# Attention loop of a hybrid decoder layer: last unit's scaling ahead of copies, next scores behind its transposes, weight splits behind the exponentials, two gate weights off GpSimd

## The chip, the cores and the metric

The kernel runs on one NeuronCore of a Trainium2 chip. Five engines work side by side, each through its own queue in order: TensorE (PE; matrix products and transposes, results in PSUM), VectorE (DVE), ScalarE (ACT), GpSimd (POOL), and SyncE (SP), which here only issues DMA transfers. They meet through semaphores. The metric is the device time of one execution in microseconds (us); the median of several runs counts.

## The reference

One layer of a hybrid decoder, on a prompt of 2048 tokens and on 8 sequences of 8 new tokens (64 sample tokens). The model width is 1024.

```python
h = rms_norm(x, g_mix_pre)
proj = jnp.einsum('btd,de->bte', h, w_in)     # 8 q heads, 2 k, 2 v heads of 64; GLA q, k, v, gate; low rank gate
q = rope(q, pos); k = rope(k, pos)
attn = swa_banded(q, k, v, sinks)             # window 128: each block of 128 queries sees 256 keys
o, s_new = gla_chunked(gq, gk, gv, log_a, s_init)
o = rms_norm(o, g_gla) * jax.nn.silu(gr)
x = x + rms_norm(concat([attn, o]) @ w_out, g_mix_post)
h = rms_norm(x, g_ffn_pre)
x = x + rms_norm(relu(h @ w_up) ** 2 @ w_down, g_ffn_post)
```

The outputs are both activations, the last keys and values of each sequence, and the states of the gated linear attention (GLA). The change touches the stage that does the first projection (q, k, v and the low rank gate) and the sliding-window attention; its softmax is

```python
m = jnp.maximum(jnp.max(scores, axis=-1, keepdims=True), sink)
p = jnp.exp(scores - m)
return p / (jnp.sum(p, axis=-1, keepdims=True) + jnp.exp(sink - m))
```

## The kernel before, in words

**Precision.** Products run in a fast 32-bit format that rounds its operands. To keep the result exact enough, an operand is split into a high part (a ScalarE copy into that format) and a low part (a VectorE subtraction: source minus high part), and a product is made of two or three matmuls (high by high, high by low, low by high). So nearly every operand costs one ScalarE copy and one VectorE subtraction: xh and xl for x, ph and pl for the softmax weights, qh and ql for the two halves of q, kh and kl for k, vv for v, wg for the gate weights.

**The attention loop** (from line 794 on) runs over 16 blocks i of 128 tokens. A block has four units u = 0 to 3; a unit is two query heads of one key head (`unit`, line 465). A unit goes through the steps: a copy of the sink (POOL), scores `sc` (four matmuls), masking with minimum (two VectorE operations, s<-sc), exponentials (two on ScalarE, with the row sum in `den`), reciprocal and scaling of s (for units 0 and 3 one head is scaled on ScalarE and one on VectorE, for units 1 and 2 both on VectorE), four transposes `pT`, the copy ph (ScalarE), the subtraction pl (VectorE), the product `av` with v (four matmuls), the copy `rest` (ScalarE) and the sum `mo` (VectorE).

The steps are written as a Python generator. In pass u the loop draws the steps of three units in turn: `behind` (the unit before, from pl to mo), `now` (from masking to ph) and `ahead` (the scores of the next unit). Between them it runs `fill`, the projection matmuls of a later block, so many as `A_FILL[u]` says in three places, 48 in a block.

**Order.** What is called through `te`, `ac` and `dv` (TensorE, ScalarE, VectorE) is chained by the class `InOrder`, so these three queues hold exactly the order in which the loop makes the calls. POOL's and SP's instructions are called plainly; a scheduler at build time places them by readiness in its own model, so POOL can start work that the loop writes later.

**Work beside the units.** It is put in by name and phase through `A_PLAN` and `do(u, phase)`; a phase is a letter, and "3A" means unit 3, phase A (behind the exponentials), "S" is behind the scaling, "B" behind the transposes, "C" behind ph, "T" behind the masking:

- `x_half(i + 3, u)` for u = 0 and 1: four transposes xT of x and their high part xh; the low part xl is the step `x0` or `x1`. It is there for i up to 13.
- `heads_T(i + 1)` in unit 2: transposes pq (q) and pk (k), their high parts, and the steps `klo0`, `klo1` (low parts of k), `lo0`, `lo1` (low parts of q on VectorE: qh<-pq and ql<-pq), `hi1` (ScalarE, ql<-pq). `lo0`, `hi1` and `klo0` are done in unit 3; `lo1` and `klo1` in unit 0 of the next block. Scores of units 0 and 1 need lo0, those of units 2 and 3 need lo1.
- `take_first(i + 2)` and `take_rest(i + 2)` (`first`, `rest`): a finished projection is taken from PSUM on ScalarE (qk, glr, vv), with the low parts of vv and glr on VectorE as step `vl`.
- `rotate(i + 1)` (`turn`): rotary embedding on POOL, five operations (tb, tb, qk, rot, rot).
- `x_norm(i + 3)` (`junk`, `rstd`): square sums.

**PSUM.** `bank` (line 168) hands out eight banks: two each of the kinds a (projections), b (scores and pk), c (pT), and one each of d and e. Kind d is used by the transposes of x and by pq, kind e by av:

```python
return ps.tile(shape, F32, tag=kind, name=name, bufs=1 if kind in "de" else 2)
```

**Gate weights.** From block 3 on two pieces of the GLA weights (chunks 0 and 1, eight pieces k each) are loaded per block into two buffers `wg_raw`, and `split_some` splits them (`split_gw`, line 257): POOL multiplies by the gain, ScalarE copies the high part, POOL subtracts for the low part. Chunks 2 and 3 (`G_LATE`), split in block 15 and later, use `split_gained`: ScalarE copies with the gain as scale, VectorE multiplies and subtracts in one operation, and POOL does nothing.

After the loop come the sample tokens, the GLA, the output projection and the MLP; nothing of them is changed.

Of the kernel before, what the change touches and what calls it, by code (L numbers as in the profile page):

```python
# [25 lines left out]
NB = T // P  # L26
# [26 lines left out]
H_FETCH = ((6, 6), (1, 0), (1, 8), (5, 0), (5, 8), (3, 0), (3, 8))  # L53
H_EARLY, H_LATE = (1, 2), (5, 7, 6, 4, 3)
G_EARLY, G_LATE = (0, 1), (2, 3)
A_FILL = ((11, 2, 0), (10, 0, 2), (10, 0, 0), (12, 1, 0))
A_LEAD, A_SPLIT = 14, (2, 1, 0, 0)
A_PLAN = [(name, (int(at[0]), at[1])) for name, at in dict(
    klo0="3T", first="1B", hi1="3C", x1="1B", lo1="0A", klo1="0B", x0="0C", rest="3A", lo0="3A", junk="2A", turn="1A", rstd="1A", vl="3S"
).items()]  # L60
G_FIRST = (0, 1)
G_NEXT = (NB, *range(2, NB))
G_ORDER = (0, 1, 2, 3)
G_FILL = (34, 14, 16, 8, 20)
# [51 lines left out]
def f32(ap):  # L116
    return ap.bitcast(F32)
# [23 lines left out]
def hybrid_step_kernel(ctx: ExitStack, tc: tile.TileContext, I, O):  # L141
# [79 lines left out]
    def split_gained(wh, wl, raw, k):  # L221

        g = gcol[:, k : k + 1]
        ac.activation(wh, raw, AF.Copy, scale=g)
        dv.scalar_tensor_tensor(wl, raw, g, f32(wh), op0=ALU.mult, op1=ALU.subtract)
# [22 lines left out]
    def open_gw(chunks):  # L248
        p_ = open_pool(f"g_w{chunks[0]}", "right")
        for c in chunks:  # L250
            gw[c] = (p_, *(p_.tile([P, KT, G_N], F32R, tag=f"w{c}{u}", name=f"wg{c}_{u}") for u in range(2)))
        return p_

    def load_gw(c, k, *stage):
        return c, k, load_raw(sp, k, G_AT + c * G_N, G_N, f"wg{c}", *stage)

    def split_gw(c, k, raw):
        if c in G_LATE:
            split_gained(gw[c][1][:, k, :], gw[c][2][:, k, :], raw, k)
            return  # L260
        nc.gpsimd.tensor_tensor(raw, raw, gcol[:, k : k + 1].to_broadcast([P, G_N]), op=ALU.mult)
        ac.activation(gw[c][1][:, k, :], raw, AF.Copy)
        nc.gpsimd.tensor_tensor(gw[c][2][:, k, :], raw, f32(gw[c][1][:, k, :]), op=ALU.subtract)
# [19 lines left out]
    def load_x(i):  # L283
        xs_in[i] = x = sp.tile([P, D], F32, tag="x", name=f"x_{i}", bufs=2)
        nc.sync.dma_start(x[: rows(i)], x_rows(i))
        ropes[i] = sp.tile([P, 2, HD], F32, tag="rope", name=f"rope_{i}", bufs=4)
        nc.sync.dma_start(ropes[i], I["c_rope"][i])
# [32 lines left out]
    def store():  # L320

        for dst, src in stores:
            nc.sync.dma_start(dst, src)
        stores.clear()
# [274 lines left out]
    def load_T(i, xT):  # L599
        for u in range(2):  # L600
            dst = xT[1][:, :, u * NS : (u + 1) * NS] if i == NB else xT[u]
            nc.sync.dma_start(f32(dst), xt_d[i][:, u])
        return xT
# [24 lines left out]
    def load_cache(name, c):  # L628
        t = sp.tile([P, 4, P], F32, tag=f"cache_{name}", name=f"c{name}_{c}", bufs=1)
        nc.sync.dma_start(t, I[f"cache_{name}"][0, c * 4 : c * 4 + 4].rearrange("b w h d -> w b (h d)"))  # L630
        return t

    def load_consts():

        raw = [gp_pool.tile([P, G_W], F32, tag="gp", name=f"c_raw{u}", bufs=2) for u in range(2)]
        nc.sync.dma_start(raw[1][:, : I["c_rest"].shape[1]], I["c_rest"])
        gk, extra = raw[0][:, :256], raw[0][:, 256:512]
        nc.gpsimd.memset(raw[0][:, :512], 0.0)
        for r0 in (0, HD):
            for a in range(3):  # L640
                nc.sync.dma_start(gk[r0 + a * 16 : r0 + a * 16 + 16], I["w_gk2"][0])
            nc.sync.dma_start(gk[r0 + 48 : r0 + 49], I["b_gk"])
            nc.sync.dma_start(extra[r0 + 49 : r0 + 50], I["b_gk"])
        wgk = kp.tile([P, 2, 256], F32R, name="wgk")
        nc.gpsimd.memset(f32(wgk), 0.0)
        for u, rr in enumerate(half_of):
            nc.scalar.activation(wgk[rr, u], gk[rr], AF.Copy)
            lo = slice(u * HD + 32, u * HD + HD)
            nc.vector.tensor_tensor(gk[lo], gk[lo], f32(wgk[lo, u]), op=ALU.subtract)
            nc.vector.tensor_tensor(wgk[lo, u], gk[lo], extra[lo], op=ALU.add)  # L650
        at = [0]

        def part(n, shape, dtype):
            t = kp.tile([n, *shape], dtype, name=f"c_{at[0]}")
            w = int(np.prod(shape))
            src = raw[1][:n, at[0] : at[0] + w]
            nc.vector.tensor_copy(t.rearrange("p a b -> p (a b)") if len(shape) > 1 else t, src)
            at[0] += w
            return t

        msk = part(P, [NL - 1, P // 4], U8)
        smsk = part(NS, [SL, NS // 2], U8)
        onehot = part(NS, [DB], F32)
        dmsk = kp.tile([P, HD], U8, name="dmsk")
        nc.vector.tensor_tensor(dmsk, ident[:, :HD], ident[:, HD:], op=ALU.add)
        ggla = bcast(kp, I["g_gla"][0], P, "ggla")
        return wgk, msk, smsk, dmsk, onehot, ggla
# [95 lines left out]
    def split_some(n):  # L763

        for _ in range(min(n, len(weights))):
            c, k, raw, stage = weights.popleft()
            split_gw(c, k, raw)
            if stage and late:
                weights.append((*load_gw(*late.popleft(), *stage), stage))
# [20 lines left out]
    now, ahead, behind = next(queue), next(queue), iter(())  # L790
# [3 lines left out]
    for i in range(NB):  # L794
        if i + 4 < NTILE:
            load_x(i + 4)
        if i == NB - 1:
            wa_pool.release()
            w_pools.append(open_gw(G_LATE))
            for n in range(4):  # L800
                stage = ("w_raw", 2) if n % 2 else ("x", 2)
                weights.append((*load_gw(*late.popleft(), *stage), stage))
        elif i >= 3:
            for _ in range(min(2, len(early))):
                weights.append((*load_gw(*early.popleft()), None))
        store()
        if i == 4:
            nc.sync.dma_start(gain_d.rearrange("a d -> (a d)"), I["g_mix_post"][0])
            wgk, msk, smsk, dmsk, onehot, ggla = load_consts()
        if i == NB - 4:  # L810
            nc.sync.dma_start(smask, I["c_smask"])
            cached.update({(name, 0): load_cache(name, 0) for name in "kv"})
        if i >= NB - 2:
            t = i - NB + 2
            gxTs[t] = load_T(t, x_place(t))
            fill = chain(fill, projecting(t, gxTs[t], G_EARLY, ac))
        new = i + 3 < NTILE
        todo["turn"] = lambda: run(rotate(i + 1))
        if i + 2 < NTILE:
            todo["first"] = lambda: take_first(i + 2)  # L820
            todo["rest"] = lambda: todo.update(vl=take_rest(i + 2))
        if new:
            todo["junk"] = lambda: todo.update(rstd=x_norm(i + 3))

        def do(u, phase):
            for name, at in A_PLAN:
                if at == (u, phase) and name in todo:
                    todo.pop(name)()

        for u in range(4):  # L830
            next(now)
            do(u, "T")
            next(behind, None)
            next(now)
            do(u, "A")
            later = next(queue)
            next(later)
            run(fill, A_FILL[u][0])
            next(behind, None)
            if u != 3:  # L840
                next(behind, None)
            run(fill, A_FILL[u][1])
            if u == 0:
                next(now)
            if u < 2 and new:
                hi, todo[f"x{u}"] = x_half(i + 3, u)
                hi()
            elif u == 2:
                todo.update(heads_T(i + 1))
            do(u, "X")  # L850
            run(fill, A_FILL[u][2])
            if u:
                next(now)
            do(u, "S")
            if u == 3:
                next(behind, None)
            next(behind, None)
            next(ahead)
            next(now)
            do(u, "B")  # L860
            split_some(A_SPLIT[u] if i < NB - 1 else 1)
            next(now)
            do(u, "C")
            behind, now, ahead = now, ahead, later
    for left in todo.values():
        left()
    store()
    fill = chain(fill, *(projecting(t, gxTs[t], G_LATE, ac) for t in G_FIRST))

# [20 lines left out]
    for n in range(4):  # L890
# [23 lines left out]
        behind, now, ahead = now, ahead, later  # L914
# [447 lines left out]
    def products():  # L1362

        xT = {G_NEXT[0]: load_T(G_NEXT[0], x_place(G_NEXT[0]))}
        for i, after in zip(G_NEXT, (*G_NEXT[1:], None)):
            if after is not None:
# [517 lines left out]
    turn = [0]  # L1884
# [304 lines left out]
```

## Time and profile before

| | |
|---|---|
| median of 3 runs | 2207.52 us (2206.16 to 2207.61) |
| profiled execution | 2206.11 us, span of the instructions 2204.0 us |
| granted TensorE clock, mean | 0.996 |
| TensorE busy | 2163.2 us, 98% of the span |
| VectorE, ScalarE, GpSimd busy | 1531.4, 1219.1, 263.0 us |
| attention loop, about 37.8 to 300 us | TensorE 256.3, VectorE 226.2, ScalarE 222.7, GpSimd 152.7 us busy of 262.2 |

A timeline row gives the start in us from the span's first instruction, the duration, the engine, the line (L130 is the helper through which the three ordered queues call), the operation, the tiles (out<-in, without buffer numbers), the shapes, and how many like instructions were merged (x2). In brackets stands the idle time before it and what ended it. A matmul's record is longer than the distance to the next one, because matmuls are pipelined; so for TensorE the distances from start to start are read. The loop's blocks are alike: in a steady block, unit 2 with pq is at 232.7 us, unit 3 from 234.1, unit 0 of the next block from 238.1, unit 1 from 242.3.

### The profile page before, as it was taken

Reading aid. Unit: us, or ns where it says so; the run is one execution under the profiler, and the core shown is the slowest. Engines: PE = TensorE matmul, PEld = TensorE weight load, DVE = VectorE, ACT = ScalarE, POOL = GpSimd, SP = SyncE. Lnnn points to the kernel's source line nnn. Section 1 sums busy time; section 2 is a strip of 40 time slices with the busy share of each in tenths; the row PEclk is TensorE's granted clock in tenths of the full one; section 3 lists DMA queues with packets and bytes.
Section 4 is the critical chain, followed back from the end, with each engine's and each line's share of the span. In section 5 each row is a group of like instructions: output and inputs, shape, how many; then the busy total and the mean of one; then the engine's idle time right before and its main releaser. Section 6 shows DMA issues by size and latency. Waiting matters only on the chain.

```text
span 2204.0 us, 34115 instructions
## 1 busy us (share of the span) xinstructions
PE 2163.2 (98%) x11784; PEld 1864.7 (85%) x11784; DVE 1531.4 (69%) x3101; ACT 1219.1 (55%) x2626; POOL 263.0 (12%) x418
## 2 busy tenths in 40 slices
PE   8999999999999999899999999999999999999998
PEld 7999989999998888688888887887888888888886
DVE  5888868777775665788888655547676666555566
ACT  5889867566664444555555544435444554444444
POOL 2566512121111100000000000000000000000000
PEclk9999999999999999999999999999999999999999
DMA  6344232214336665768777677758554334766685
GB/s 228 131 137 156 96 106 70 68 64 148 136 125 237 223 208 190 239 228 277 260 261 270 232 236 225 240 182 260 180 195 149 138 144 148 238 201 193 194 269 185
DMA packets 240185, 411.53 MB, mean 187 GB/s; under 512 B 25924, under 2 KB 142124, under 8 KB 235900
## 3 DMA queue, kind: packets, MB, share of 16 engines
q1 hardware_dynamic: 240012, 409.35, 55.9%
q8 instruction: 93, 1.52, 0.3%
q14 instruction: 80, 0.66, 0.1%
HBM read 265.82 MB, written 143.99 MB: 186 GB/s over the span
## 4 chain that ended last, share of the span: by engine, by line
PE 85%; DVE 6%; ACT 4%; DMA 2%; issue 1%; POOL 1%; SPq 0%; DVEq 0%; ACTq 0%; POOLq 0%
PE dn L130 26%; PE gproj L130 10%; PE uc L130 7%; PE ua L130 7%; PE out L1318 6%; PE proj L130 5%; PE ue L130 4%; PE ud L130 4%; PE ub L130 4%; PE av L130 1%; PE sam L130 1%; PE dsam L130 1%; PE o L130 1%; PE pT L130 1%; PE sc L130 1%
## 5 line engine op out<-in xcount | busy, mean ns | idle before, releaser
L130 PE MATMUL dn<-o0t,o0s 128*128 128x512 f32 x896 | 349.3, 390 | 2.8 <-DVE f L1891 1.5
L130 PE MATMUL dn<-o1t,o0s 128*128 128x512 f32 x896 | 349.5, 390 | 0.3 <-DVE o1t L219 0.2
L130 PE MATMUL dn<-o0t,o1s 128*128 128x512 f32 x896 | 349.4, 390 | 0.0
L219 DVE TENSOR_TENSOR o1s<-rs,o0s 128x512 fp32r<-128x512 f32 x224 | 154.7, 691 | 227.8 <-ACT o0s L218 223.7
L218 ACT ACTIVATE o0s<-rs 128x512 fp32r<-128x512 f32 x224 | 141.1, 631 | 305.5 <-PE dn L130 282.3
L130 PE MATMUL gproj<-wg,gxh 128*128 128x384 f32 x1024 | 272.5, 342 | 0.3 <-DVE gp_s L213 0.3
L130 ACT ACTIVATE st<-st 128x512 f32<-128x512 f32 x224 | 141.2, 630 | 140.7 <-DVE st L130 136.6
L130 PEld LDWEIGHTS dn<-o0t,o0s 128*128 128x128 f32 x896 | 168.3, 188 | 40.6 <-DVE f L1891 2.4
L130 PEld LDWEIGHTS dn<-o1t,o0s 128*128 128x128 f32 x896 | 168.2, 188 | 37.0 <-DVE o1t L219 1.1
L130 PEld LDWEIGHTS dn<-o0t,o1s 128*128 128x128 f32 x896 | 168.2, 188 | 35.0
L130 PEld LDWEIGHTS gproj<-wg,gxh 128*128 128x128 f32 x1024 | 183.8, 188 | 4.1 <-issue 3.1
L130 PE MATMUL uc<-H,s 128*128 128x512 f32 x768 | 186.8, 391 | 0.4 <-DVE s L130 0.4
L130 PE MATMUL gproj<-wg,gxl 128*128 128x384 f32 x576 | 186.0, 340 | 0.2 <-DVE gp_s L213 0.2
L130 PE MATMUL ua<-H,w 128*128 128x512 f32 x744 | 179.2, 390 | 0.0
L130 PEld LDWEIGHTS uc<-H,s 128*128 128x128 f32 x768 | 142.9, 188 | 31.2 <-DVE s L130 0.8
L130 PEld LDWEIGHTS ua<-H,w 128*128 128x128 f32 x744 | 139.7, 188 | 29.5
L1318 PE MATMUL out<-wo,mt 128*128 128x512 f32 x680 | 158.6, 392 | 0.0
L219 DVE TENSOR_TENSOR o1t<-rt,o0t 128x512 fp32r<-128x512 f32 x224 | 153.5, 685 | 7.0 <-ACT o0t L218 6.9
L208 POOL TENSOR_TENSOR frs<-rs_v,half 128x1 f32<-128x1 f32 (+1 forms) x13 | 10.1, 787 | 1214.4 <-DVE rs_v L206 694.5
L1318 PEld LDWEIGHTS out<-wo,mt 128*128 128x128 f32 x680 | 126.5, 188 | 26.1
L218 ACT ACTIVATE o0t<-rt 128x512 fp32r<-128x512 f32 x224 | 138.3, 618 | 8.9 <-DMA rt<-t_d 7.2
L130 DVE TENSOR_TENSOR st<-st 128x512 f32<-128x512 f32 x160 | 110.6, 692 | 27.0 <-ACT st L130 22.6
(405 smaller groups left out, 4322.3 us busy)
## 6 DMA issues: line engine op xcount, KB each, us to landing
s_d<-st SPq DMA_DIRECT2D x32, 1792.0 KB, 8.7
rs<-s_d SPq DMA_DIRECT2D x224, 256.0 KB, 2.8
raw<-in_w_up SPq DMA_DIRECT2D x64, 512.0 KB, 4.3
rt<-t_d SPq DMA_DIRECT2D x128, 256.0 KB, 4.1
rt<-in_w_down SPq DMA_DIRECT2D x96, 256.0 KB, 3.1
t<-in_w_down SPq DMA_DIRECT2D x64, 256.0 KB, 4.0
t_d<-t SPq DMA_DIRECT2D x32, 512.0 KB, 3.2
hraw<-h_d SPq DMA_DIRECT2D x20, 512.0 KB, 5.1
```

What stands on the lines that cost most here:

```text
L130: ins = call(*a, **k)
L208: nc.gpsimd.tensor_tensor(out, v[:n], e, op=ALU.pow)
L218: nc.scalar.activation(hi, src, AF.Copy)
L219: vector.tensor_tensor(lo, src, f32(hi), op=ALU.subtract)
L1318: te.matmul(banks[c], x, w[:, c * 512 : (c + 1) * 512], start=k + u == 0, stop=k == KT - 1 and u == len(products) - 1,)
```

## The change

Five things are moved or replaced; what is computed stays.

1. In unit 3 the scaling comes ahead of `take_rest` and `lo0` (steps `rest` and `lo0` from "3A" to "3S"), and the scores of the next unit come behind the transposes of unit 3 instead of ahead of them.
2. Two of unit 0's eleven first projection matmuls go to unit 3, between av and the transposes.
3. `lo1` goes from "0A" (ahead of unit 0's scaling) to "0S" (behind it, and behind the transposes of x in the order of the calls), and `x0` from "0C" to "1A", behind pl of unit 0; in block 0 it stays.
4. The splits of gate weights go from behind the transposes to behind the exponentials, and from units 0 and 1 (two and one) to units 1 and 2; block 15 keeps its place.
5. Pieces 2 and 3 of chunk 0, which are split in block 4, use `split_gained`.

```diff
-A_FILL = ((11, 2, 0), (10, 0, 2), (10, 0, 0), (12, 1, 0))
-A_LEAD, A_SPLIT = 14, (2, 1, 0, 0)
+A_FILL = ((9, 2, 0), (10, 0, 2), (10, 0, 0), (12, 3, 0))
+A_LEAD, A_SPLIT = 14, (0, 2, 1, 0)
 A_PLAN = [(name, (int(at[0]), at[1])) for name, at in dict(
-    klo0="3T", first="1B", hi1="3C", x1="1B", lo1="0A", klo1="0B", x0="0C", rest="3A", lo0="3A", junk="2A", turn="1A", rstd="1A", vl="3S"
+    klo0="3T", first="1B", hi1="3C", x1="1B", lo1="0S", klo1="0B", x0="1A", rest="3S", lo0="3S", junk="2A", turn="1A", rstd="1A", vl="3S"
 ).items()]
+G_GAINED = ((0, 2), (0, 3))
...
     def split_gw(c, k, raw):
-        if c in G_LATE:
+        if c in G_LATE or (c, k) in G_GAINED:
             split_gained(gw[c][1][:, k, :], gw[c][2][:, k, :], raw, k)
             return
...
             for name, at in A_PLAN:
+                if name == "x0" and i == 0:
+                    at = 0, "C"
                 if at == (u, phase) and name in todo:
                     todo.pop(name)()
...
             next(now)
             do(u, "A")
+            if i < NB - 1:
+                split_some(A_SPLIT[u])
             later = next(queue)
...
             next(behind, None)
-            next(ahead)
+            if u != 3:
+                next(ahead)
             next(now)
+            if u == 3:
+                next(ahead)
             do(u, "B")
-            split_some(A_SPLIT[u] if i < NB - 1 else 1)
+            if i == NB - 1:
+                split_some(1)
             next(now)
```

## The prediction

> **What bounds the kernel now.** I read the page first (busy shares), then the windows of the stages, then the timeline of one attention block, engine by engine, because each engine's queue there has an order written by hand. The page's first part and the window from 37.8 to 300 us, which is the attention loop that the change rewrites (columns: PE, PEld, DVE, ACT, POOL busy, granted clock, DMA share, GB/s):
>
> ```profile
> PE 2163.2 (98%) x11784; PEld 1864.7 (85%) x11784; DVE 1531.4 (69%) x3101; ACT 1219.1 (55%) x2626; POOL 263.0 (12%) x418
> 37.80:300.00 262.20, 256.27 (x1699) 240.36 (x1698) 226.17 (x676) 222.70 (x613) 152.66 (x273) 0.99 0.38 128
> ```
>
> TensorE sets the pace, but in this loop VectorE (86%) and ScalarE (85%) are nearly as full, so a moved instruction soon makes TensorE wait. TensorE records 5.9 us of idle time here; small waits hide inside long matmul records, so I read them from start to start. One steady block, ScalarE:
>
> ```profile
> 230.62 0.60 ACT L130 ACTIVATE ph<-pT 128x512 fp32r<-128x512 f32 x1 [0.19 <-PE pT L130]
> ...
> 236.14 0.19 ACT L130 ACTIVATION_READ_ACCUMULATOR s<-s,m 128x1 f32 x1
> 236.24 0.45 ACT L130 ACTIVATE qk<-proj,rstd_all 128x248 f32<-128x248 f32 x1
> ...
> 236.75 0.37 ACT L130 ACTIVATE vv<-proj,rstd_all 128x128 fp32r<-128x128 f32 x1
> 237.03 0.51 ACT L130 ACTIVATE s<-s,den 128x256 f32<-128x256 f32 x1
> 237.56 0.38 ACT L130 ACTIVATE rest<-av 64x256 f32<-64x256 f32 x1
> 238.38 0.60 ACT L130 ACTIVATE ph<-pT 128x512 fp32r<-128x512 f32 x1 [0.44 <-PE pT L130]
> ...
> 239.63 0.51 ACT L130 ACTIVATE s<-s,m 128x257 f32<-128x257 f32 x1
> ...
> 240.54 0.19 ACT L130 ACTIVATION_READ_ACCUMULATOR s<-s,m 128x1 f32 x1
> ...
> 247.02 0.60 ACT L130 ACTIVATE ph<-pT 128x512 fp32r<-128x512 f32 x1 [0.19 <-PE pT L130]
> ```
>
> From the copy ph of unit 1 (230.62) to the next block's (247.02) is the period, 16.40 us. Up to 236.33, where the exponentials of unit 3 end, ScalarE waits for nothing. So a delay of that copy passes whole into the next block; I measure the change there. VectorE, same block:
>
> ```profile
> 236.82 0.17 DVE L130 RECIPROCAL den<-den 128x2 f32<-128x2 f32 x1
> 237.03 0.83 DVE L130 TENSOR_SCALAR s<-s,den 128x256 f32<-128x256 f32 x1
> 237.77 0.34 DVE L130 SCALAR_TENSOR_TENSOR vv<-proj,rstd_all,vv 128x128 fp32r<-128x128 f32 x1
> ...
> 238.28 0.42 DVE L130 TENSOR_TENSOR mo<-av,rest 64x256 f32<-64x256 f32 x1
> 238.74 0.48 DVE L130 CUSTOM_DVE_ANT_0 s<-sc,amask,sink 128x256 f32<-128x256 f32 x1
> ...
> 239.55 0.69 DVE L130 TENSOR_TENSOR pl<-pT,ph 128x512 fp32r<-128x512 f32 x1
> 240.27 0.69 DVE L130 SCALAR_TENSOR_TENSOR ql<-pq,ql 64x512 fp32r<-64x512 f32 x1
> ...
> 241.19 0.56 DVE L130 TENSOR_SCALAR s<-s,den 128x256 f32<-128x256 f32 x1
> ...
> 242.56 0.69 DVE L130 TENSOR_TENSOR xl<-xT,xh 128x512 fp32r<-128x512 f32 x1
> ...
> 245.07 0.62 DVE L130 TENSOR_SCALAR s<-s,den 128x256 f32<-128x256 f32 x2
> ```
>
> TensorE, same block, and the one place where block 1 shows a hidden tie (the last three rows, the first of them VectorE's):
>
> ```profile
> 232.22 0.28 PE L130 MATMUL av<-ph,vv 128*128 128x256 f32 x1
> 232.34 0.39 PE L130 MATMUL av<-pl,vv 128*64 128x256 f32 x2
> ...
> 236.74 0.34 PE L130 MATMUL proj<-wa_lo,xh 128*128 128x392 f32 x1
> ...
> 237.59 0.75 PE L130 MATMUL pT<-ident,s 128*128 128x128 f32 x4
> ...
> 240.87 0.34 PE L130 MATMUL proj<-wa_hi,xl 128*128 128x392 f32 x1
> 241.05 0.62 PE L130 MATMUL xT<-ident,x 128*128 128x128 f32 x4
> ...
> 241.99 0.60 PE L130 MATMUL pT<-ident,s 128*128 128x128 f32 x4
> ...
> 244.22 0.28 PE L130 MATMUL av<-ph,vv 128*128 128x256 f32 x1
> 244.71 0.45 PE L130 MATMUL av<-pl,vv 128*64 128x256 f32 x2 [0.21 <-DVE rs_v L130]
> ```
> ```profile
> 56.54 0.69 DVE L130 SCALAR_TENSOR_TENSOR ql<-pq,ql 64x512 fp32r<-64x512 f32 x1
> 57.03 0.34 PE L130 MATMUL proj<-wa_hi,xl 128*128 128x392 f32 x1
> 57.33 0.63 PE L130 MATMUL xT<-ident,x 128*128 128x128 f32 x4
> ```
>
> Two waits are there to win: the av product at 244.71 comes 0.49 after its predecessor instead of 0.12 (232.22 to 232.34; it waits for VectorE's pl: 0.37 lost), and the transposes at 237.59 last 0.75 instead of 0.60 (they wait for the scaled s). The tie: bank d, a single PSUM buffer, holds pq until the last reader has done, and the next block's first x transposes (xT) write it. That last reader is the VectorE step lo1, ql<-pq. In block 1 xT starts 0.30 behind its predecessor instead of the usual 0.18, and 0.10 after ql ends (57.23); in the block above xT (241.05) again follows ql's end (240.96) by 0.09. The bank is freed just in time.
>
> **The change part by part.** I replay the block above with the new order; times are those of that block.
>
> *Unit 3.* take_rest and lo0 go behind the scaling. The reciprocal no longer waits behind lo0: 236.36 instead of 236.82. Reciprocal to scaling is 0.20, so both halves start at 236.56; ScalarE's ends at 237.07. VectorE's half took 0.83, while POOL's rotation ran beside it, which take_rest's first copy releases; that copy is now later, so I take 0.31 (half the pair at 245.07): done 236.9. Then lo0 (0.69, the form of ql): 237.6. ScalarE: take_rest takes 0.88 to the end of vv, now 237.97; then rest of unit 2 to 238.26.
>
> TensorE has three projection matmuls instead of one (0.18 each, 241.05-240.87) before the transposes: 236.74 + 0.54 = 237.28, no wait. The next scores follow at 237.67, just after lo0. The 0.25 us lost at 237.59 go; the two extra projections were taken from unit 0, so TensorE's work is unchanged.
>
> VectorE then needs vv: the two low parts and the sum mo take 0.97 (238.74-237.77) from 238.0, so the next unit's masking starts at 238.97, 0.23 later than now. ScalarE: ph at 238.28, 0.10 earlier, and the exponentials end at 240.63 instead of 240.73.
>
> *Unit 0, the moved lo1.* pl of unit 3 follows the masking by 0.81: 239.78 to 240.47. TensorE, with nine projections instead of eleven, reaches the av product that needs it at about 239.96 (the scores 0.56, as 241.05 to 241.99 less the four transposes; nine projections 1.6; one av matmul 0.12): a wait of 0.55. From there to xT it is three av matmuls and two projections, some 0.74, so TensorE reaches xT at 241.24. But lo1 now stands behind the scaling: reciprocal 240.66, scaling 240.86, lo1 from its end. The scaling took 0.56 beside POOL's last rotation steps; beside the middle ones, where it will now lie, no row shows it. The ends are 0.31 (nothing beside) and 0.83 (beside the first steps); I take 0.57, the row of this same instruction. So lo1 runs 241.45 to 242.14 and xT starts at 242.19: TensorE stands for 0.95, and xT is 1.14 later than now.
>
> *Unit 1.* x0 (xl, 0.69) goes behind pl, so pl is ready before av asks: the 0.37 lost now go. xl itself ends at 245.8, and the second x transposes, which need bank d again, come at 245.9: 0.1 to spare; without that they would wait instead. The scaling of unit 1 ends some 0.2 before its transposes. So ph of unit 1 comes 1.14 - 0.37 = 0.77 later: 247.79, and the period grows by 0.77. Blocks 1 to 13 have both lo1 and x transposes: 13 x 0.77 = +10.0 us. With the scaling at its ends, 0.51 to 1.03 per block: +6.6 to +13.4.
>
> [...]
>
> *Weight splits and the two gained weights.* In block 4 the ScalarE copies wait for POOL's multiplication, which stands behind the rotation, and TensorE for them:
>
> ```profile
> 109.63 0.52 ACT L130 ACTIVATE wg<-wg_raw 128x384 fp32r<-128x384 f32 x1 [2.04 <-POOL wg_raw L261]
> 111.47 0.38 PE L130 MATMUL av<-ph,vv 128*128 128x256 f32 x1 [1.82 <-ACT ph L130]
> 109.51:112.92 3.41, 1.24 (x8) 0.91 (x8) 1.20 (x5) 2.62 (x8) 3.33 (x5) 1.00 0.13 28
> 112.92:116.33 3.41, 3.41 (x16) 3.41 (x15) 2.30 (x8) 1.92 (x5) 1.32 (x3) 0.50 0.88 283
> 723.91:727.32 3.41, 1.83 (x13) 1.39 (x12) 2.82 (x5) 2.12 (x6) 1.05 (x2) 1.00 0.98 313
> L130 DVE SCALAR_TENSOR_TENSOR wg<-wg_raw,gcol,wg x16: 609/614/679, 290.3 to 322.8; 128x384 fp32r<-128x384 f32 x16
> ```
>
> TensorE loses the 1.82 and, in the stretch at clock 0.50 that follows, half of 3.41, 1.7: together 3.5. Chunk 0's weights 2 and 3 are the ones split there. They no longer need POOL's multiplication and subtraction (four instructions fewer), and the wait goes: -3.5. In their place VectorE gets two subtractions of 0.61 ahead of unit 1's reciprocal, where it has 0.2 spare: +1.2 at most, which I take; 0 at least. Net -2.3. In blocks 5 to 10 the two copies (0.52 each) go from unit 0 to behind the exponentials of unit 1, ahead of rest; ScalarE waited 0.48 there and the average copy is long done before ph. POOL's two subtractions, SP's refills and POOL's two multiplications come some 2 us later, but are wanted a block later: 0, and if POOL is late once more, up to the 2.04 above per block. POOL's rotation starts 0.8 later; its result is wanted by the next unit 2: 0. The stores and x loads behind the refills on SP serve the next block: 0. Blocks 0, 14 and 15 have no moved lo1 ahead of x transposes: 0, give or take 1.
>
> Sum: +10.0 - 2.3 = +7.7 on the profiled execution (2206.1 us, span 2204.0, 2.1 around it): 2213.8. The median of the runs, 2207.5, is 1.4 above that execution, so 2215.2. Its own range: +6.6 - 3.5 to +13.4 - 0, rounded: 2211 to 2221.
>
> **The rivals.** *B, no change.* The x transposes are not held, because lo1 still comes in time. Then unit 0 keeps the 0.55 at av and wins the 0.25 and the 0.37: -0.07 per block, -1 in all, and with -2.3 about 2204.3. For it: ends of ScalarE steps overlap by 0.1, and lo1 was in time so far. Against it: the exponentials end at 240.6, and three VectorE steps follow in a row.
>
> *C, faster.* VectorE's chain into unit 0 runs unhindered: the masking starts when its scores are there (238.15: the first pair takes 0.2 and 0.28 from 237.67) instead of 238.97, and the scaling takes its short 0.31. Then lo1 ends 0.82 + 0.26 earlier, at 241.06, and the period changes by 0.77 - 1.08 = -0.31: 13 times, -4.0, with -2.3: 2201.2. It decides where lo1 ends in the block above: at 241.5 the sum is even, at 241.2 or before the gain can be measured. Against it: the low part of vv must follow ScalarE's take_rest, at 237.97, and mo follows that.
>
> *D, slower still.* The two waits in unit 0 (0.55 and 0.95) lie within 1.8 us of each other and halve the clock. The stretch with TensorE busy for 1.24 of 3.41 us was followed by clock 0.50, the one with 1.83 (723.91) was not; with 1.50 idle the new stretch has 1.91 busy. If it halves in each block, 13 x 1.7 = +22: 2237; in a third of them, 2222. [...] A POOL multiplication late in blocks 5 to 10 (6 x 2.04 = +12) would give 2227.
>
> **How the numbers follow.** My forecast 0.65, B 0.18, C 0.06, D 0.11. A measurement of this kernel can tell about 0.2% (4.4 us) from no change: faster below 2203.1, slower above 2211.9. Faster is C with a little of B, 0.07; same is the rest of B with the low edge of mine, 0.19; slower 0.74. The range reaches down into B and up to D's start: 2205 to 2223.
>
> **What would show it.** After the change, right: xT of unit 0 starting 0.05 to 0.1 after ql ends in every block with a gap near 0.9 before it; period near 17.2 between ph copies of unit 1; no wait of av in unit 1; unit 3's scaling on VectorE near 0.35; block 4 without the 1.82 us wait and no clock 0.50 near 113. Wrong: xT without a gap (B), period under 16.4 (C), clock 0.50 in stretches of the loop (D), ScalarE waiting for POOL's wg_raw in blocks 5 to 10.

## The result, and the profile after

The changed kernel is slower: 2218.53 us in the median of five runs (2215.68 to 2223.62), against 2207.52 for the kernel before; the ratio is 1.0053, 95% interval 1.0042 to 1.0064. That is some 11.7 us by the ratio. The forecast was 2215.2 with 2205 to 2223. The profiled execution is the slowest of the five, 2223.62 us with a span of 2221.8, so what follows compares stretches of the loop, not whole executions.

First the attention loop as one window, from 37.8 us to ph of unit 1 in block 15, before and then after (columns: length of the window, then PE, PEld, DVE, ACT and POOL busy, granted clock, DMA share, GB/s):

```profile
37.80:294.39 256.59, 250.66 (x1663) 235.15 (x1662) 221.52 (x661) 217.93 (x599) 152.66 (x273) 0.99 0.38 129
```
```profile
37.80:306.61 268.81, 253.49 (x1660) 235.28 (x1659) 217.99 (x663) 219.62 (x599) 147.43 (x268) 0.98 0.36 123
```

The same work ends 12.2 us later. VectorE and GpSimd are busy for less time than before, ScalarE for 1.7 us more and TensorE for 2.8; TensorE's idle time grows from 5.9 to 15.3, so most of the time is not in longer work but in gaps. Which gaps, TensorE's waits in the loop of the changed kernel say (total us, times, longest):

```profile
PE xT L131 <- DVE ql L131: 8.4, 13, 1.6
PE av L131 <- DVE pl L131: 4.7, 15, 0.6
```

The x transposes wait for ql once in each of thirteen blocks; before, no such line stood there. One steady block without weight splits, changed kernel, timeline, TensorE first, then VectorE, GpSimd and ScalarE:

```profile
248.83 0.28 PE L131 MATMUL av<-ph,vv 128*128 128x256 f32 x1
249.39 0.45 PE L131 MATMUL av<-pl,vv 128*64 128x256 f32 x2 [0.28 <-DVE pl L131]
...
249.97 0.34 PE L131 MATMUL proj<-wa_hi,xh 128*128 128x392 f32 x1
250.89 0.66 PE L131 MATMUL xT<-ident,x 128*128 128x128 f32 x4 [0.58 <-DVE ql L131]
...
254.08 0.27 PE L131 MATMUL av<-ph,vv 128*128 128x256 f32 x1
254.19 0.40 PE L131 MATMUL av<-pl,vv 128*64 128x256 f32 x2
...
254.56 0.63 PE L131 MATMUL xT<-ident,x 128*128 128x128 f32 x4
```
```profile
245.47 0.35 DVE L131 TENSOR_SCALAR s<-s,den 128x256 f32<-128x256 f32 x1
...
249.77 0.35 DVE L131 TENSOR_SCALAR s<-s,den 128x256 f32<-128x256 f32 x1
250.14 0.69 DVE L131 SCALAR_TENSOR_TENSOR ql<-pq,ql 64x512 fp32r<-64x512 f32 x1
...
253.73 0.68 DVE L131 TENSOR_TENSOR xl<-xT,xh 128x512 fp32r<-128x512 f32 x1
...
254.58 0.62 DVE L131 TENSOR_SCALAR s<-s,den 128x256 f32<-128x256 f32 x2
```
```profile
249.89 1.36 POOL L401 TENSOR_TENSOR rot<-qk,tb 128x512 f32<-128x512 f32 x1
```
```profile
239.54 0.60 ACT L131 ACTIVATE ph<-pT 128x512 fp32r<-128x512 f32 x1 [0.20 <-PE pT L131]
...
256.50 0.60 ACT L131 ACTIVATE ph<-pT 128x512 fp32r<-128x512 f32 x1 [0.20 <-PE pT L131]
```

ql runs from 250.14 to 250.83 and xT starts 0.06 later: the bank is handed over the moment its last reader has done. From the projection before it to xT it is 0.92, where 0.18 is usual, so TensorE stands for 0.74. The period is 16.96 (before: 16.40). In blocks 5 to 10, which split weights, it is 17.33; block 1 took 19.31 (before 16.56), and block 4 took 17.76 (before 19.86).

### The profile page after: what moved, and what is told of

Same layout as the page of the kernel before. It is cut to its first block, busy times and chain, and to the rows that moved or that the text cites. A ratio compares the mean times of both kernels' runs of the same rounds, so it can differ in the third digit from the quotient of the medians.

```text
span 2221.8 us, 34114 instructions
## 1 busy us (share of the span) xinstructions
PE 2168.3 (98%) x11784; PEld 1866.4 (84%) x11784; DVE 1527.2 (69%) x3103; ACT 1218.8 (55%) x2626; POOL 258.4 (12%) x414
## 3 DMA queue, kind: packets, MB, share of 16 engines
q8 instruction: 93, 1.52, 0.3%
## 4 chain that ended last, share of the span: by engine, by line
PE 80%; DVE 7%; ACT 7%; DMA 3%; issue 2%; POOL 1%; SPq 0%; DVEq 0%; ACTq 0%; POOLq 0%
PE dn L131 26%; PE gproj L131 9%; PE uc L131 7%; PE ua L131 7%; PE out L1327 6%; PE ud L131 4%; PE ub L131 4%; PE ue L131 4%; PE proj L131 3%; ACT s L131 2%; PE sam L131 1%; PE dsam L131 1%; PE o L131 1%; DVE s L131 1%; DMA rt<-t_d 1%
```

## The experiments

Each is given by its edit, against the changed kernel unless it says otherwise. Their traces are compared by the period (ph of unit 1 to ph of unit 1 a block later; without splits and with), and by the time of that copy in block 15, where the loop is all but over. "Ratio" is to the kernel before.

| kernel | period, no splits / splits | block 4 | ph in block 15 | ratio, 95% interval |
|---|---|---|---|---|
| before | 16.40 / 16.41 | 19.86 | 294.4 | 1 |
| changed | 16.97 / 17.33 | 17.76 | 306.6 | 1.0053, 1.0042 to 1.0064 |
| e1: lo1 back | 16.81 / 17.12 | 17.54 | 299.9 | 1.0036, 1.0023 to 1.0048 |
| e2: lo1 alone (on before) | 17.69 / 17.69 | 19.45 | 311.5 | 1.0072, 1.0057 to 1.0087 |
| e3: xT in another bank | 16.17 / 16.65 | 17.08 | 293.9 | 1.0001, 0.9991 to 1.0010 |
| e4: gained weights alone (on before) | 16.42 / 16.43 | 18.03 | 293.4 | 1.0003, 0.9993 to 1.0012 |
| e5: splits back | 16.97 / 17.37 | 18.55 | 306.9 | 1.0061, 1.0046 to 1.0075 |
| e6: no gained weights | 16.97 / 17.35 | 20.98 | 310.4 | 1.0066, 1.0052 to 1.0080 |
| e7: e3, splits back | 16.13 / 16.34 | 17.67 | 292.3 | 0.9993, 0.9985 to 1.0002 |
| e8: e3, all gained | 16.13 / 17.10 | 17.10 | 297.1 | 1.0016, 1.0006 to 1.0026 |
| e9: e3, one split per unit | 16.15 / 18.6 to 19.6 | 18.86 | 307.0 | 1.0062, 1.0049 to 1.0074 |
| e10: scores behind alone (on before) | 17.09 / 17.08 | 20.87 | 303.5 | 1.0044, 1.0031 to 1.0057 |
| e11: x0 alone (on before) | 16.12 / 16.41 | 19.92 | 294.8 | 1.0006, 0.9997 to 1.0015 |

The fifth column goes with the fourth: the rest of the execution adds a few us either way. For e9 the second period is that of blocks 5 to 9; block 10 took 16.37.

**Is it the bank, or only lo1's place on VectorE?** Three runs: the step back in its old place, the step moved alone, and the order of the change with unit 0's x transposes in the bank of the probabilities, so that they need not wait for ql.

```diff
-    ..., x1="1B", lo1="0S", klo1="0B", ...
+    ..., x1="1B", lo1="0A", klo1="0B", ...
```


> The changed kernel with one part undone: lo1 is again ahead of unit 0's scaling (phase 0A). Theory (bank d is held until lo1 has read pq, so TensorE's x transposes of blocks 1 to 13 wait for lo1): xT of unit 0 has its normal distance of about 0.18 us again, the period of a block without weight splits falls from 16.97 to about 16.4, and the time to about 2207 (2204 to 2211), 10 to 12 us under the changed kernel. Rival (the loss comes from the weight splits behind the exponentials, VectorE beside POOL, and halved clocks): xT's gap is gone but the time stays at 2214 or more.


```diff
-    ..., x1="1B", lo1="0A", klo1="0B", ...      (kernel before)
+    ..., x1="1B", lo1="0S", klo1="0B", ...
```


> The kernel before with only one part of the change: lo1 behind unit 0's scaling (phase 0S). Theory: xT of unit 0 waits 0.6 to 0.9 us for lo1 in blocks 1 to 13; 13 times about 0.7, so about 2216 (2213 to 2220). Rival (the splits and POOL): within 2 us of 2207.5.


```diff
-                hi, todo[f"x{u}"] = x_half(i + 3, u)
+                hi, todo[f"x{u}"] = x_half(i + 3, u, "c" if u == 0 else "d")
```


> The changed kernel as it is, lo1 still behind the scaling, but the first x transposes of a block write a bank of kind c (two buffers, shared with pT) instead of the single bank d. Theory (it is the bank, not lo1's place on VectorE): no wait of xT for lo1, and the time falls to about 2206 (2203 to 2211). Rival (lo1 behind the scaling delays VectorE's later steps whatever the bank): 2214 or more, with the wait moved to another step of unit 0 or 1. A second rival inside the theory: xT0 in bank c takes a buffer that pT needs, and pT of unit 0 or 1 waits instead.

e3 decides. VectorE's order is untouched, and the loss is gone: 1.0001, with a period of 16.17, below that of the kernel before. The wait at pT that the second rival looked for doesn't show. Its timeline (TensorE, then VectorE) shows the transposes starting at the moment at which ql only begins:

```profile
238.67 0.34 PE L131 MATMUL proj<-wa_hi,xh 128*128 128x392 f32 x1
238.85 0.60 PE L131 MATMUL xT<-ident,x 128*128 128x128 f32 x4
```
```profile
238.86 0.69 DVE L131 SCALAR_TENSOR_TENSOR ql<-pq,ql 64x512 fp32r<-64x512 f32 x1
```

e2 is the same cause from the other side: the step moved alone costs 1.29 per block, more than was expected of it (a median of 2221.4 us for 2213 to 2220), and TensorE's waits (kernel before with that one step moved) name it:

```profile
PE xT L130 <- DVE ql L130: 15.5, 12, 1.3
```

e1 missed what was expected of it. The wait for ql is gone there, yet the period is 16.81 and not back at 16.4, and the median is 2213.2 us for 2204 to 2211. With lo1 ahead of it the scaling comes later, and falls into GpSimd's rotation; the steps of unit 1 on VectorE follow later too (timeline of e1, VectorE, then GpSimd, then TensorE):

```profile
244.62 1.02 DVE L131 TENSOR_SCALAR s<-s,den 128x256 f32<-128x256 f32 x1
...
247.87 0.68 DVE L131 TENSOR_TENSOR xl<-xT,xh 128x512 fp32r<-128x512 f32 x1
```
```profile
244.20 1.29 POOL L401 TENSOR_TENSOR rot<-qk,tb 128x512 f32<-128x512 f32 x1
```
```profile
248.29 0.28 PE L131 MATMUL av<-ph,vv 128*128 128x256 f32 x1
248.70 0.63 PE L131 MATMUL xT<-ident,x 128*128 128x128 f32 x4
```

The second x transposes now come 0.41 behind av, where the changed kernel has 0.14 (254.42 to 254.56): they wait until xl, the last reader of the first ones in the same bank, has ended (248.55). Against e3 TensorE loses some 0.3 there, and another 0.3 before it at pT of unit 0 and av of unit 1, whose operands come late by the scaling. In the changed kernel the same scaling starts at 249.77, 0.12 before that operation of GpSimd (249.89), and takes 0.35. So lo1's two places cost this order by different waits, and putting it back gives back only a third of the loss by the ratio, about half by the copy in block 15.

**The parts that were to win.** The two gained weights alone, the third part alone (next scores, `rest`, `lo0` and the two fills of unit 3), and `x0` alone, each on the kernel before; and the changed kernel without the gained weights.

```diff
+G_GAINED = ((0, 2), (0, 3))                      (kernel before)
...
-        if c in G_LATE:
+        if c in G_LATE or (c, k) in G_GAINED:
```


> The kernel before with only the two gained weights (chunk 0, pieces 2 and 3, split without POOL). Theory: block 4 loses its wait of 1.82 us and the half clock stretch behind it, and pays up to 1.2 for the two VectorE operations: 2.3 less, about 2205 (2204 to 2207.5). Rival: the wait in block 4 has another cause (the load of the weights) and stays: 2207.5, clock 0.50 near 113 us still there.


```diff
-G_GAINED = ((0, 2), (0, 3))
+G_GAINED = ()
```


> The changed kernel, with all early gate weights on GpSimd again (G_GAINED empty). If the two weights that left GpSimd are worth what block 4 showed (17.76 now for 19.86 before), block 4 goes back to about 19.9 with the clock at 0.50 near 113 us, and the time rises by about 2 us, to 2220.5. The rival, by what those two weights did alone on the kernel before (a shorter block 4, and no time in the end), leaves the time within 1 us of the changed kernel's.


```diff
-A_FILL = ((11, 2, 0), (10, 0, 2), (10, 0, 0), (12, 1, 0))     (kernel before)
+A_FILL = ((9, 2, 0), (10, 0, 2), (10, 0, 0), (12, 3, 0))
-    ..., rest="3A", lo0="3A", ...
+    ..., rest="3S", lo0="3S", ...
-            next(ahead)
+            if u != 3:
+                next(ahead)
             next(now)
+            if u == 3:
+                next(ahead)
```


> The kernel before with the third part of the change alone: in unit 3 the next scores behind the transposes (with the q parts and the filling matmuls that go along). The prediction refunds 0.25 us per block for it: a period of 16.15 for 16.40, and 13 x 0.25 = 3.2 us less, about 2203. The rival, that the wait it ends only moves to the next unit, keeps 16.40 and the time of the kernel before.


```diff
-    ..., x0="0C", ...                            (kernel before; block 0 keeps "0C")
+    ..., x0="1A", ...
```


> The kernel before with the low part of the first x half moved alone (from the end of unit 0 to unit 1). The prediction refunds 0.37 us per block for it, by the wait of unit 1's last matmuls: 16.03 for 16.40, and 13 x 0.37 = 4.8 us less, about 2201. The rival, that VectorE's order only passes the wait on to unit 1's scaling or to the second x transposes, leaves 16.4 or more.

The gained weights do what they should: block 4 is 1.83 shorter, and without them the changed kernel loses 3.2 in block 4 and 1.8 in block 5, where clock 0.50 follows the wait. On the time of e4 it can't be seen (1.0003), and the interval of e6 overlaps that of the changed kernel. e10 is a plain miss: not 0.25 won but 0.68 lost in each block. The wait at unit 3's transposes is gone. But the masking of unit 0 comes 0.19 later, and GpSimd's rotation, which waits for a ScalarE copy that now stands behind unit 3's scaling, 0.67 later; so VectorE's scaling of unit 0 comes 0.40 after the start of that operation instead of 0.88, and takes 1.04 for 0.56 (timeline of e10, VectorE, then GpSimd):

```profile
247.84 1.04 DVE L130 TENSOR_SCALAR s<-s,den 128x256 f32<-128x256 f32 x1
```
```profile
247.44 1.29 POOL L400 TENSOR_TENSOR rot<-qk,tb 128x512 f32<-128x512 f32 x1
```

e11 wins 0.3 in blocks 2, 11 and 12 and nothing in those with splits, and it loses 1.3 in block 1 (17.90), where TensorE waits 1.0 and 0.7 for VectorE; that block was not followed further. So the two refunds of the forecast aren't sums that can be had one by one.

**The splits.** The changed kernel with its splits back where they were; the same on top of e3; e3 with all early weights off GpSimd; and e3 with the splits spread, at most one per unit (two weights come per block, so they fall in units 0 and 1).

```diff
-            if i < NB - 1:
-                split_some(A_SPLIT[u])
...
-            if i == NB - 1:
-                split_some(1)
+            split_some((2, 1, 0, 0)[u] if i < NB - 1 else 1)
```


> The changed kernel, with the weight splits back in their old places (two in unit 0 and one in unit 1, behind the transposes of the unit). The theory of a collision says that in blocks 5 to 10 VectorE's scaling of unit 1 is long (1.14 us) only because the two splits of unit 1, where the change put them, send GpSimd's subtraction beside it: the scaling goes back to about 0.35, the period of these blocks from 17.33 to the 16.97 of the blocks without splits, and the time falls by 6 x 0.36 = 2.2 us, to about 2216. The rival, that a split costs the new order 0.36 wherever it stands, because VectorE has no slack left behind the wait of the first x transposes, keeps 17.33 and about 2218.5.

> The changed kernel with unit 0's x transposes in the bank of the probabilities (as before), and the splits back in their old places besides. If the splits cost only by their place, blocks 5 to 10 come down from 16.65 to the 16.2 of the blocks without splits, 6 x 0.45 = 2.7 us: about 2203, under the kernel before (2205.6 to 2207.5). The rival, that splits cost this order 0.45 anywhere, gives 2206. A second rival: in their old place they run beside the rotation on GpSimd, which then ends later, and the time is 2208 or more.


```diff
-G_GAINED = ((0, 2), (0, 3))                      (on top of e3)
+G_GAINED = tuple((c, k) for c in G_EARLY for k in range(KT))
```


> The changed kernel with unit 0's x transposes in the bank of the probabilities, and all sixteen early gate weights split by ScalarE and VectorE alone, none on GpSimd. If the 0.45 us in blocks 5 to 10 is GpSimd's subtraction beside VectorE's scaling (1.08 for 0.35 us), it goes: a period near 16.2 and about 2203. The rival, that VectorE's own order is what paces these blocks, puts two further subtractions of about 0.6 us each in front of unit 1's scaling: up to 0.5 us more than now in six blocks, about 2209.


```diff
-A_LEAD, A_SPLIT = 14, (0, 2, 1, 0)               (on top of e3)
+A_LEAD, A_SPLIT = 14, (1, 1, 1, 0)
```


> The changed kernel with unit 0's x transposes in the bank of the probabilities, and its three splits one each in units 0, 1 and 2, still behind the unit's exponentials. After the runs with the splits put back, the theory is that a split costs by two engines: ScalarE's two weight copies (0.41 us each) in front of the next copy of the probabilities, or GpSimd's subtraction (1.01) beside VectorE's scaling. With one copy in each of ScalarE's pauses neither should be whole: a period of 16.2 to 16.4 in blocks 5 to 10 for 16.65, and 2203 to 2205. The rival, that one subtraction beside unit 1's scaling is enough for the whole loss (the second of the two lies behind it anyway), keeps 16.65 and 2206.

Why blocks with splits take 0.36 more in the changed kernel, its own timeline shows (VectorE, GpSimd, ScalarE):

```profile
220.28 1.14 DVE L131 TENSOR_SCALAR s<-s,den 128x256 f32<-128x256 f32 x1
...
221.94 0.67 DVE L131 TENSOR_TENSOR xl<-xT,xh 128x512 fp32r<-128x512 f32 x1
```
```profile
220.26 1.01 POOL L264 TENSOR_TENSOR wg<-wg_raw,wg 128x384 fp32r<-128x384 f32 x1 [1.79 <-ACT wg L131]
...
221.80 1.01 POOL L264 TENSOR_TENSOR wg<-wg_raw,wg 128x384 fp32r<-128x384 f32 x1
```
```profile
219.67 0.92 ACT L131 ACTIVATE wg<-wg_raw 128x384 fp32r<-128x384 f32 x2
...
221.86 0.59 ACT L131 ACTIVATE qk<-proj,rstd_all 128x392 f32<-128x392 f32 x1 [0.24 <-POOL rstd_all L209]
222.35 0.59 ACT L131 ACTIVATE ph<-pT 128x512 fp32r<-128x512 f32 x1
```

The first of the two scalings of unit 1 takes 1.14, where the pair took 0.62 in the other block: GpSimd's subtraction of the weights began 0.02 before it. That delay reaches the period in two parts. Some 0.15 come ahead of ph: its transposes take 0.67 for 0.60, and ScalarE's copy qk, which stands ahead of it, waits 0.24 for the normalisation factor, which stands behind that subtraction on GpSimd. The other 0.23 come behind ph: the masking of unit 2 follows the late scaling on VectorE, and ScalarE starts the next exponentials 0.70 behind ph instead of 0.49. Block 3, the first with such a split, has 0.15 more than a block without, and block 11, behind the last, 0.22. e5 takes the long scaling away (the pair is at 0.62 again), and yet its period stays at 17.37: the rival had the number, though not by a lack of slack on VectorE. In the old place ScalarE's two copies stand ahead of ph, which comes 1.32 behind xh instead of 0.91 (timeline of e5, first a block with splits, then one without):

```profile
182.84 0.60 ACT L131 ACTIVATE xh<-xT 128x512 fp32r<-128x512 f32 x1 [0.81 <-PE xT L131]
183.34 0.93 ACT L131 ACTIVATE wg<-wg_raw 128x384 fp32r<-128x384 f32 x2
184.16 0.59 ACT L131 ACTIVATE ph<-pT 128x512 fp32r<-128x512 f32 x1
...
251.89 0.60 ACT L131 ACTIVATE xh<-xT 128x512 fp32r<-128x512 f32 x1 [0.80 <-PE xT L131]
252.80 0.60 ACT L131 ACTIVATE ph<-pT 128x512 fp32r<-128x512 f32 x1 [0.31 <-PE pT L131]
```

So each place has its own price, by another engine. With the bank free (e7), where xh comes earlier, the old place costs 0.2 instead of e3's 0.48; its ratio of 0.9993 can't be told from the kernel before. e8 takes GpSimd out of the splits altogether, and the scaling is short; but VectorE has its two subtractions ahead of the reciprocal, and the period rises to 17.10, as that run's rival said:

```profile
212.59 1.15 DVE L131 SCALAR_TENSOR_TENSOR wg<-wg_raw,gcol,wg 128x384 fp32r<-128x384 f32 x2
213.66 0.16 DVE L131 RECIPROCAL den<-den 128x2 f32<-128x2 f32 x1
213.85 0.62 DVE L131 TENSOR_SCALAR s<-s,den 128x256 f32<-128x256 f32 x2
```

e9 went worse than either theory had it. A buffer of weights is refilled once GpSimd's subtraction has read it, and that stands behind the rotation; GpSimd's own queue then reaches the next multiplication before the transfer has landed, the normalisation factor stands behind that, and ScalarE waits for the factor (12.3 us in all, 1.2 in e3). Two stretches at clock 0.50, at 172 and 192 us, fall into blocks 8 and 9. From e9's waits between 114 and 209 us, GpSimd's and then ScalarE's:

```profile
POOL wg_raw L262 <- DMA wg_raw<-in_w_in: 17.0, 10, 2.1
```
```profile
ACT qk L131 <- POOL rstd_all L209: 12.3, 5, 2.8
```

None of the versions beats the kernel before by more than can be measured.

## Why the prediction was right, and where it was not

The sign, the cause and the place were right; the steady loss was put too high, block 1 too low, and the weight splits were put at nothing. From ph in block 0 to ph in block 13 the profiled execution lost 9.7 us (216.75 to 226.42) where the sum had 7.7. That the two are this near is in part luck: 0.57 for 0.77 in thirteen blocks is -2.6, the splits in blocks 5 to 10 are +2.2, and block 1 is +2.2 above a steady block; the rest is small.

- *The bank* (+0.95 of TensorE standing): measured 0.74 in blocks 2 to 13 (0.90 to 0.92 from start to start, less the usual 0.18) and more in block 1, with xT 0.06 behind ql in all thirteen. The missing 0.2 is the scaling, next. e3 shows that it is the bank. Rivals B and C fall with it. The gap repeats in thirteen blocks, and with another bank it doesn't show.
- *Unit 0's scaling* (0.57 taken between ends of 0.31 and 0.83): 0.35. This is the whole difference in a block without splits, 0.57 for 0.77. The ends were no two speeds of that instruction. It ran fast because it began 0.12 ahead of GpSimd's rotation; in block 14 it began 0.14 behind it and took 1.30.
- *The wait at av for pl* (0.55): 0.44, that is 0.56 from start to start less the usual 0.12. *No wait of av in unit 1* (0.37 won): 0.11 from start to start there. *Second x transposes with 0.1 to spare*: xl ends at 254.41 and xT starts at 254.56. In e1, where they do wait, they also start 0.15 behind the end of xl (248.55, 248.70), so nothing was to spare. *Unit 3's scaling* (0.31 taken): 0.35. So the refunds came as the replay had them, but e10 and e11 show that they hang on the rest of the order: alone, one is a loss.
- *Weight splits, costed at nothing*: this step failed. The text looked for a late multiplication on GpSimd and for ScalarE's two copies, and did not set GpSimd's subtraction against VectorE's scaling of unit 1, nor against the normalisation factor behind it. Measured: 0.36 in each of six blocks, +2.2.
- *Block 4* (0.77 - 2.3 = -1.5): -2.1; no wait for GpSimd and no clock 0.50 near 113 us, as foreseen.
- *Block 1* (+0.77): +2.75. VectorE carries the constants of a later stage there (1.12, before 0.60) and its scaling falls into the rotation (0.98), so xT waits 1.6. Rival D, which was priced for many blocks, came true in this one, and again in block 1 of e5 and e6 (clock 0.50 from 59.5 and 58.2). Its windows (columns as above) show it:

```profile
56.79:60.20 3.41, 1.69 (x12) 1.37 (x13) 2.23 (x5) 1.63 (x6) 2.49 (x6) 1.00 0.00 0
60.20:63.61 3.41, 3.41 (x15) 3.41 (x14) 2.41 (x9) 1.97 (x6) 0.56 (x3) 0.50 0.00 0
```

  A stretch with 1.69 us busy was followed by clock 0.50; of the forecast's two, the one with 1.24 was and the one with 1.83 was not. Busy time alone draws no line between these: in e7 a stretch with 1.80 (from 921.15) was followed by it, in e1 one with 1.52 (from 731.56) was not. Behind the steady blocks' two waits the clock stayed at 1.00 (from 63.6 to 739.4 us), as the forecast assumed.
- *Blocks 0, 14 and 15* (0, give or take 1): +0.6, +1.4 and +0.55. Block 0 may be chance: e5, with the same order there, is at 46.48 (before 46.54, changed 47.14), and of all kernels of the table only this execution spent 6.8 us at clock 0.50 from 36.3 us, the others 3.4. In block 14 the scaling of unit 0 took 1.30 for 0.55 before, 0.75 of the 1.4; the rest was not followed.

After the loop the profiled execution lost another 5.6 us. The code there is the same, but it has 13.7 us at clock 0.50 there (three stretches, at 739, 917 and 931 us) where the kernel before had 6.8 (at 905 and 915), not counting one at the very end of both, and over all kernels of the table the time from ph in block 15 to the end lies anywhere from 1908 to 1915 us. That such stretches made up the last microseconds of the miss in the median (2218.5 for 2215.2) is likely and not shown.

## What to carry to other kernels

When a step that reads PSUM is moved, ask who writes that buffer next and when: with a single buffer per kind the reader's place in its own queue is a due time for another engine (here xT started 0.06 us behind ql in thirteen blocks), and giving the writer another bank may be all that the new order lacks. Price each moved instruction against what runs on GpSimd at its new time, not by its mean (here one scaling of VectorE took from 0.35 to 1.30 us), and expect parts of a reordering to be worth something else alone than together. Before a step that frees a load's buffer is put off, see when that buffer is refilled and what queues behind the wait for it.

## What the runs showed of the hardware that was not expected

VectorE's scaling (one tensor times a value per row, SBUF to SBUF) isn't slowed by GpSimd in proportion. Where it starts inside a two-tensor operation of GpSimd on 320 to 512 columns, and not in the last 0.05 us of it, it ends 0.14 to 0.18 us after that operation, however long that still lasts, in all 56 cases of 128x256 scalings that the loops of the kernels before and after have. It does so begun 0.02 after that operation's start in the changed kernel (220.26 + 1.01 = 221.27; the scaling ends at 221.42), 0.42 after it in e1 (245.49, ends 245.64), and 0.40 after it in e10 (248.73, ends 248.88). So did the 0.56 of the kernel before, whose GpSimd row is

```profile
240.31 1.29 POOL L400 TENSOR_TENSOR rot<-qk,tb 128x512 f32<-128x512 f32 x1
```

(241.60, and the scaling ended at 241.75). Started 0.12 earlier than such an operation, in the last 0.04 us of the one before (249.77 in the changed kernel), it takes 0.35; so it does beside GpSimd's operation on a single column (128x1; 237.61). The subtraction xl, which reads one of its inputs from PSUM, isn't touched: at 221.94 it took 0.67 beside GpSimd's 221.80, and 0.68 at 253.73, beside no such operation. What ties the scaling to GpSimd the traces don't show; they show that some tenths of a microsecond in the order decide: 0.35 us for the scaling begun 0.12 ahead of the rotation's operation, 1.30 for the one begun 0.14 behind it (284.05 in the changed kernel). On GpSimd's side less shows: the operation begun 0.12 behind the scaling took 1.36 for 1.29, though the scaling had 0.23 to go.
